# Hybrid decoder step on one core: keys and attention queries transposed two heads at a time instead of from doubled copies

## The chip, the core and the metric

The kernel runs on 1 core of one Trainium2 chip. The time is device microseconds (us) of one execution of the whole program. Five engines work side by side and wait for one another only through semaphores: TensorE (PE, with its weight loads shown apart as PEld), VectorE (DVE), ScalarE (ACT), GpSimd (POOL) and SyncE (SP, which here only issues DMAs). Each runs its own instructions strictly in the order in which they stand.

## The reference

One decoder layer for a prompt of 2048 tokens and 8 decode sequences of 8 tokens. What matters here is the attention of the prompt: 8 query heads and 4 key/value heads of 64 dimensions, so two query heads share a key head.

```python
def sparse_attend(q, kg, vg, valid):
    qg = q.reshape(B, T, N_KV_HEADS, N_HEADS // N_KV_HEADS, HEAD_DIM)
    s = jnp.einsum('btgrd,btkgd->btgrk', qg, kg, ...) * HEAD_DIM ** -0.5
    s = jnp.where(valid[:, :, None, None, :], s, -jnp.inf)
    p = jax.nn.softmax(s, axis=-1).astype(vg.dtype)
    o = jnp.einsum('btgrk,btkgd->btgrd', p, vg)
...
    score = indexer_scores(qib, wb, ki)          # 8 indexer heads, one shared key
    idx, valid = select_keys(score, posb, k_top) # 256 best causal keys of each query
    return sparse_attend(qb, take(k, idx), take(v, idx), valid)
```

The kernel computes the attention densely over all causal keys and adds a mask that leaves the selected ones. Around it stand the input projection, a gated position mixing, the output projection and a last gated projection.

## The kernel before

The program has three stages. **Stage A** (`phase_a`, 0 to about 1026 us) projects the 17 blocks of 128 tokens, scores and selects keys (the indexer) and, at its end, multiplies the gated mixing by one half of the output weights (`gm_product`, lines 585 to 589, 34 products). **Stage B** (`phase_b`, about 1026 to 1516 us) is the attention of the prompt; the decode sequences' attention is mixed in between as filler. **Stage C** (`phase_c`, to the end) is the output projection and the gated one behind it.

All products are in float32r with the operands split in a high part and a low part (`split`, lines 124 to 127: ACT copies the high part out of PSUM, DVE subtracts it to get the low part). For the scores the split is laid over the partitions: a head has 64 dimensions, TensorE has 128 rows. `Kst` holds for each key head the high part of the transposed keys in partitions 0 to 63 and the low part in 64 to 127. A transposed query head stands in both halves, so one matmul multiplies it with the high and the low part of the keys together: `b_qh` is the high part of the query doubled, `b_ql` its low part doubled (lines 1117 and 1118).

To have every head doubled, the kernel before transposes inputs that are doubled already. `load_q` (line 1009) reads the 128x512 queries of a block twice into `b_qr`, in pieces of 64 numbers, so that each head's 64 columns stand there twice; `prep_q` (line 1043) then makes 8 transposes of 128x128 into two PSUM banks and splits each bank. `twice` (line 1027) lets ACT copy a block of keys doubled into `b_kd`; `prep_kv` (line 1031) makes 4 transposes into one bank, ACT copies the bank to `Kst`, DVE replaces the lower half by the difference; POOL splits the values into `Vst`. Key and value blocks are loaded two ahead (pool `b_raw` with two buffers).

`prep_early` prepares the queries of block 0 and all 16 key blocks while the last products of stage A run on PE. In stage B a block i of queries is worked in four steps g = 0 to 3, one per key head, each with two heads: `scores` (matmuls into the pool `b_s` of two banks, then DVE adds the mask and takes the running extreme, ACT exponentiates) and, one step later, `values` (transposes of the probabilities into the pool `b_tp` of four banks, a split by ACT and DVE into `b_pt`, then the product with `Vst`). The queries of the next block are prepared at the end of step g = 2, in banks of the same pool `b_tp`, and the load of the block after it is issued right there. Between the stages A and B stands a conditional block (`fallback`, line 915) that every engine has to pass.

The order on each engine is set by a scheduler when the program is built: it plays the program with its own estimate of durations and puts down what is ready. The code above gives it dependencies and priorities; on the chip each engine keeps to that order.

## Time and profile before

| | |
|---|---|
| runs | 1872.78, 1873.06, 1878.46 us; median 1873.06 us |
| profiled execution | 1874.53 us, of it 1872.7 us span from the first to the last instruction |
| mean granted TensorE clock | 0.991 of 2.4 GHz |
| busy, share of the span | PE 97%, PEld 85%, DVE 66%, ACT 54%, POOL 32% |
| DMA | 261.54 MB in all |
| stage B, 1050 to 1520 us | PE 459.80, DVE 411.86, ACT 373.44, POOL 153.29 of 470 us |

A share is an average over stages that differ: DVE is 66% busy over the span, and 88% in stage B. A matmul's listed duration is longer than the step from one to the next, since they are pipelined; what a matmul costs PE is read from the start of the next one. An engine's idle time is put down to the event that ended it.

### The profile page before, as it was taken

The page shows a single profiled execution, that of the slowest core. Times are in us where ns is not written, and L with a number is a line of the kernel's source. Part 1 is how long each engine was busy: PE and PEld are TensorE (multiplying, and loading weights), DVE is VectorE, ACT ScalarE, POOL GpSimd, SP SyncE. Part 2 cuts the span into 40 slices and gives each one's busy share as a digit, 9 for nine tenths or more (in the row PEclk, how much of TensorE's full clock was granted, in tenths as well). Part 3 has the DMA queues.
Part 4 walks back from the last instruction along what each step waited for, and adds up shares of the span by engine and source line. Part 5 has one row for each costly group of instructions (what it writes and reads, how often), then busy time and mean ns, then how long its engine had stood idle before and what let it go on. Part 6 is the DMA issues. An engine that isn't in the chain of part 4 may idle for free. (4 is left out here: it accounts for less than half of the span.)

```text
span 1872.7 us, 33926 instructions
## 1 busy us (share of the span) xinstructions
PE 1821.9 (97%) x11974; PEld 1599.1 (85%) x11974; DVE 1243.2 (66%) x3638; ACT 1019.7 (54%) x1912; POOL 608.2 (32%) x967
## 2 busy tenths in 40 slices
PE   7998999999999999999999899999999999999998
PEld 6997978999999999998988777788778878888887
DVE  4588753568788638768754788899979974233321
ACT  3234434446656636677665888688867753122121
POOL 4566362433013325004403642522234113222221
PEclk9998999999999999999999899999999999999999
DMA  8854665645445564454455551522133063223211
GB/s 241 283 182 145 212 204 188 212 126 157 127 154 167 201 185 144 142 169 154 151 195 169 144 138 49 157 63 72 54 87 116 12 226 109 75 96 107 93 37 46
DMA packets 243807, 261.54 MB, mean 140 GB/s; under 512 B 83177, under 2 KB 209841, under 8 KB 243249
## 3 DMA queue, kind: packets, MB, share of 16 engines
q1 hardware_dynamic: 147200, 144.10, 24.8%
q10 hardware_dynamic: 90544, 96.35, 15.8%
q0 software_dynamic: 5888, 18.88, 3.5%
q8 instruction: 95, 1.56, 0.3%
q14 instruction: 80, 0.65, 0.1%
HBM read 171.90 MB, written 87.37 MB: 138 GB/s over the span
## 5 line engine op out<-in xcount | busy, mean ns | idle before, releaser
L323 PE MATMUL z<-whi,hhi 128*128 128x256 f32 (+1 forms) x1792 | 463.4, 292 | 7.6 <-ACT qn L397 2.6
L324 PE MATMUL z<-wlo,hhi 128*128 128x256 f32 (+1 forms) x1792 | 454.4, 287 | 1.3 <-DVE wlo L293 1.3
L323 PEld LDWEIGHTS z<-whi,hhi 128*128 128x128 f32 x1792 | 342.1, 191 | 17.2 <-ACT qn L397 3.6
L324 PEld LDWEIGHTS z<-wlo,hhi 128*128 128x128 f32 x1792 | 342.4, 191 | 6.5 <-DVE wlo L293 1.5
L326 PE MATMUL z<-whi,hlo 128*128 128x256 f32 (+1 forms) x1792 | 262.1, 285 | 0.0
L326 PEld LDWEIGHTS z<-whi,hlo 128*128 128x128 f32 x1792 | 237.9, 189 | 2.2
L706 DVE SCALAR_TENSOR_TENSOR big<-dots,sgn,big 128x1024 f32<-128x1024 f32 (+7 forms) x176 | 179.0, 1017 | 48.2 <-ACT dots L704 43.1
L127 DVE TENSOR_TENSOR b_pt<-b_tp,b_pt 128x512 fp32r<-128x512 f32 (+1 forms) x288 | 183.3, 655 | 12.8 <-ACT b_pt L126 11.7
L1169 PE MATMUL b_o<-b_pt,Vst 128*128 128x512 f32 x544 | 184.0, 421 | 1.3 <-DVE b_pt L127 1.3
L704 ACT ACTIVATE dots<-dots 128x1024 f32<-128x1024 f32 (+7 forms) x176 | 139.7, 800 | 82.3 <-PE dots L702 78.5
L126 ACT ACTIVATE b_pt<-b_tp 128x512 fp32r<-128x512 f32 (+1 forms) x288 | 156.5, 579 | 43.2 <-PE b_tp L1152 39.3
L1152 PE MATMUL b_tp<-mats,b_sm 128*128 128x128 f32 x1088 | 170.8, 275 | 1.6 <-ACT b_sm L1126 0.7
L843 ACT ACTIVATE bfw<-big,tk 128x384 bf16<-128x384 f32 (+14 forms) x105 | 136.5, 1300 | 60.3 <-DVE tk L863 34.9
L1126 ACT ACTIVATE b_sm<-b_sm,b_st 128x128 f32<-128x128 f32 (+15 forms) x128 | 154.9, 1211 | 24.3 <-DVE b_st L1119 23.6
L1152 PEld LDWEIGHTS b_tp<-mats,b_sm 128*128 128x128 f32 x1088 | 132.3, 141 | 31.0 <-ACT b_sm L1126 3.3
L1117 PE MATMUL b_s<-Kst,b_qh 128*128 128x512 f32 (+3 forms) x320 | 138.3, 435 | 5.1 <-DVE b_st L1119 4.3
L1119 DVE CUSTOM_DVE_ANT_0 b_sm<-b_s,b_mask,b_st 128x512 f32<-128x512 f32 (+3 forms) x192 | 123.8, 645 | 18.4 <-PE b_s L1118 13.9
L701 PE MATMUL dots<-ki_stack,qih 128*128 128x512 f32 (+3 forms) x304 | 113.1, 373 | 3.4 <-DVE big L706 1.8
L1118 PE MATMUL b_s<-Kst,b_ql 128*128 128x512 f32 (+3 forms) x320 | 116.4, 368 | 0.0
L702 PE MATMUL dots<-ki_stack,qil 128*128 128x512 f32 (+3 forms) x304 | 109.4, 369 | 0.0
L1169 PEld LDWEIGHTS b_o<-b_pt,Vst 128*128 128x128 f32 x544 | 91.0, 190 | 20.9 <-DVE b_pt L127 5.5
L1484 PE MATMUL c_mm<-c_h_w_ple_gate,c_mh 128*128 128x512 f32 x272 | 108.8, 400 | 0.0
(349 smaller groups left out, 3742.7 us busy)
## 6 DMA issues: line engine op xcount, KB each, us to landing
whi<-s_wh ACTq DMA_DIRECT2D x52, 512.0 KB
wlo<-s_wl ACTq DMA_DIRECT2D x52, 512.0 KB
raw<-w_in SPq DMA_DIRECT2D x112, 128.0 KB
s_wh<-whi ACTq DMA_DIRECT2D x13, 1024.0 KB
s_wl<-wlo ACTq DMA_DIRECT2D x13, 1024.0 KB
s_r<-hlo SPq DMA_DIRECT2D x32, 256.0 KB
b_qr<-s_q SPq DMA_DIRECT2D x32, 256.0 KB
c_r<-s_r SPq DMA_DIRECT2D x16, 512.0 KB
```

Source lines behind the costliest of these rows:

```text
L126: nc.scalar.activation(hi, src, AF.Copy)
L127: nc.vector.tensor_tensor(lo, src, hi.bitcast(F32), OP.subtract)
L323: nc.tensor.matmul(z, lhsT=hh[:, k], rhs=wh[:, k, :n], start=(k == 0), stop=False)
L324: nc.tensor.matmul(z, lhsT=hh[:, k], rhs=wl[:, k, :n], start=False, stop=False)
L326: nc.tensor.matmul(z, lhsT=hl[:, k], rhs=wh[:, k, :n], start=False, stop=(k == 7))
L704: nc.scalar.activation(r, r, AF.Relu)
L706: nc.vector.scalar_tensor_tensor(a, r, self.sgn[:, b, h:h + 1], a, op0=OP.mult, op1=OP.add)
L843: nc.scalar.activation(junk, acc[:P], AF.Sign, bias=cur[:, 0:1], accum_out=cur[:, 1:2])
L1117: nc.tensor.matmul(ps, lhsT=qh[:, h], rhs=rhs, start=True, stop=False)
L1126: nc.scalar.activation(part, part, AF.Exp, bias=stt[:, h, c:c + 1], scale=-1.0, accum_out=stt[:, h, 4 + e:5 + e])
L1152: nc.tensor.transpose(ps[:, k, r], sm2[r][:, (k0 + k) * 128:(k0 + k) * 128 + 128], ident)
L1169: nc.tensor.matmul(o.rearrange("p a b -> p (a b)"), lhsT=Vst[:, kb, g].rearrange("p a d -> p (a d)"), rhs=pt[:, k].rearrange("p a b -> p ( ...
```

## The change

Heads are no longer doubled ahead of the transposes. A transpose of 128 columns takes two heads at once: the first comes out in partitions 0 to 63, the second in 64 to 127. The doubling is done behind it, by copies that cross the halves:

- Queries (`prep_q`, new function `heads`): one load of 128x512 in whole rows, 4 transposes into one bank. For each of the two heads of a pair (e = 0, 1) ACT copies 64x512 to the head's own half of `b_qh`, DVE subtracts to the own half of `b_ql`, ACT copies the same source to the other half of `b_qh`, and the other half of `b_ql` is made by DVE out of the bank for blocks 0 to 4, and by POOL as a copy in SBUF for blocks 5 to 15. That is 4 ACT instructions of 64x512 for 2 of 128x512, and 4 or 2 DVE instructions of 64x512 for 2 of 128x512, and 0 or 2 on POOL.
- Keys (`prep_kv`): 2 transposes of the loaded keys, no doubled copy. For an even key head the high part stays in the upper half, for an odd one in the lower; ACT copies 64x256 and DVE subtracts 64x256, each twice per block.
- Key and value blocks are loaded four ahead (pool `b_raw` with four buffers).
- The queries of the next block are prepared at the end of step g = 0 instead of g = 2, and with them the load of the block after it is issued two steps earlier.
- The indexer's heads are transposed doubled, as before.

```diff
--- before.py
+++ after.py
@@ -44,6 +44,8 @@
 KIN = 4
 LAG_SM = 4
 LEAD = 2
+QR = 1
+AHEAD = 4
 SPS = 0
 SY = 8
 X_POOL = 0
@@ -673,6 +675,20 @@
             n = min(512, W - c)
             self.nc.gpsimd.tensor_scalar(acc[:P, c:c + n], self.iota[:P, :n], float(c), -UNIT, op0=OP.add, op1=OP.mult)
 
+    def heads(self, pool, names, ps, bufs, direct):
+        nc = self.nc
+        qh, ql = (pool.tile([128, 2, 4, 128], F32R, name=n, bufs=bufs) for n in names)
+        own = [slice(0, 64), slice(64, 128)]
+        for e in range(2):
+            nc.scalar.activation(qh[own[e], e], ps[own[e]], AF.Copy)
+            nc.vector.tensor_tensor(ql[own[e], e], ps[own[e]], qh[own[e], e].bitcast(F32), OP.subtract)
+            nc.scalar.activation(qh[own[1 - e], e], ps[own[e]], AF.Copy)
+            if direct:
+                nc.vector.tensor_tensor(ql[own[1 - e], e], ps[own[e]], qh[own[e], e].bitcast(F32), OP.subtract)
+            else:
+                nc.gpsimd.tensor_scalar(ql[own[1 - e], e], ql[own[e], e].bitcast(F32), 1.0, 1.0, op0=OP.mult, op1=OP.mult)
+        return qh, ql
+
     def idx(self, b):
         nc, wk, wk2 = self.nc, self.wk, self.wk2
         W = 128 * (b + 1)
@@ -988,7 +1004,7 @@
         qp = pool("b_q", 2)
         tiny = pool("b_tiny", 3)
         er = ExitStack()
-        raw = er.enter_context(tc.tile_pool(name="b_raw", bufs=2, reuse_waits="tile", side="right"))
+        raw = er.enter_context(tc.tile_pool(name="b_raw", bufs=AHEAD, reuse_waits="tile", side="right"))
         Kst = self.Kst = [kv.tile([128, 4, 512], F32R, name=f"Kst{c}") for c in range(4)]
         Vst = self.Vst = kv.tile([128, NB, 4, 2, 64], F32R, name="Vst")
         cm = kv.tile([128, 256], BF, name="cm")
@@ -1007,10 +1023,9 @@
             kvs[i] = (k, v)
 
         def load_q(i):
-            q = io.tile([128, 8, 2, 64], F32, name="b_qr", bufs=1)
+            q = io.tile([128, 4, 128], F32, name="b_qr", bufs=QR)
             ga = io.tile([128, 512], F32, name="b_ga")
-            for a in range(2):
-                nc.sync.dma_start(q[:, :, a], self.s_q[i].rearrange("t (h d) -> t h d", h=8))
+            nc.sync.dma_start(q, self.s_q[i].rearrange("t (h d) -> t h d", h=4))
             nc.sync.dma_start(ga, self.s_ga[i])
             qs[i] = (q, ga)
 
@@ -1022,39 +1037,32 @@
             else:
                 self.ms[i] = cm[:, 256 - W:]
 
-        kds = {}
-
-        def twice(i):
-            kds[i] = raw.tile([128, 4, 2, 64], F32, name="b_kd")
-            nc.scalar.copy(kds[i], kvs[i][0].rearrange("p (h d) -> p h d", h=4)[:, :, None, :].to_broadcast([128, 4, 2, 64]))
-
         def prep_kv(i, psum):
-            k, v = kds.pop(i), kvs.pop(i)[1]
+            k, v = kvs.pop(i)
             ps = psum()
-            for g in range(4):
-                nc.tensor.transpose(ps[:, g], k[:, g].rearrange("p a d -> p (a d)"), ident)
-            ks = Kst[i // 4][:, :, (i % 4) * 128:(i % 4) * 128 + 128]
-            nc.scalar.activation(ks, ps, AF.Copy)
-            V.tensor_tensor(ks[64:128], ps[64:128], ks[64:128].bitcast(F32), OP.subtract)
+            for j in range(2):
+                nc.tensor.transpose(ps[:, j], k[:, j * 128:j * 128 + 128], ident)
+            ks = Kst[i // 4].rearrange("p (j e) n -> p j e n", e=2)[:, :, :, (i % 4) * 128:(i % 4) * 128 + 128]
+            own = [slice(0, 64), slice(64, 128)]
+            for e in range(2):
+                nc.scalar.activation(ks[own[e], :, e], ps[own[e], 0:2], AF.Copy)
+                V.tensor_tensor(ks[own[1 - e], :, e], ps[own[e], 0:2], ks[own[e], :, e].bitcast(F32), OP.subtract)
             vv = v.rearrange("p (g d) -> p g d", g=4)
             nc.gpsimd.tensor_scalar(Vst[:, i, :, 0], vv, 1.0, 1.0, op0=OP.mult, op1=OP.mult)
             nc.gpsimd.tensor_tensor(Vst[:, i, :, 1], vv, Vst[:, i, :, 0].bitcast(F32), OP.subtract)
 
         def prep_q(i, psum):
             q, ga = qs.pop(i)
-            qh = qp.tile([128, 8, 128], F32R, name="b_qh")
-            ql = qp.tile([128, 8, 128], F32R, name="b_ql")
-            for j in range(2):
-                ps = psum()
-                for h in range(4):
-                    nc.tensor.transpose(ps[:, h], q[:, j * 4 + h].rearrange("p a d -> p (a d)"), ident)
-                self.split(qh[:, j * 4:j * 4 + 4], ql[:, j * 4:j * 4 + 4], ps)
+            ps = psum()
+            for j in range(4):
+                nc.tensor.transpose(ps[:, j], q[:, j], ident)
+            qh, ql = self.heads(qp, ("b_qh", "b_ql"), ps, 2, i < 5)
             stt = tiny.tile([128, 8, 6], F32, name="b_st")
             self.prs[i] = (qh, ql, ga, stt)
 
         self.load_q, self.load_mask, self.prep_q = load_q, load_mask, prep_q
-        load_kv(0)
-        load_kv(1)
+        for i in range(AHEAD):
+            load_kv(i)
         load_q(ORDER[0])
         for b in ORDER[:2]:
             if b < 2:
@@ -1062,14 +1070,11 @@
         yield
         prep_q(ORDER[0], psum)
         load_q(ORDER[1])
-        twice(0)
         yield
         for i in range(NB):
-            if i + 1 < NB:
-                twice(i + 1)
             prep_kv(i, psum)
-            if i + 2 < NB:
-                load_kv(i + 2)
+            if i + AHEAD < NB:
+                load_kv(i + AHEAD)
             yield
         er.close()
 
@@ -1110,12 +1115,12 @@
                         sm = both[:, r, :W]
                     out.append(sm)
 
-                    def chunk(c, h=h, sm=sm):
+                    def chunk(c, h=h, sm=sm, r=r):
                         c0, cn = c * 512, min(512, W - c * 512)
                         ps = sp.tile([128, 512], F32, name="b_s")[:, :cn]
                         rhs = Kst[c][:, g, :cn]
-                        nc.tensor.matmul(ps, lhsT=qh[:, h], rhs=rhs, start=True, stop=False)
-                        nc.tensor.matmul(ps, lhsT=ql[:, h], rhs=rhs, start=False, stop=True)
+                        nc.tensor.matmul(ps, lhsT=qh[:, r, g], rhs=rhs, start=True, stop=False)
+                        nc.tensor.matmul(ps, lhsT=ql[:, r, g], rhs=rhs, start=False, stop=True)
                         V.tensor_tensor_reduce(out=sm[:, c0:c0 + cn], in0=ps, in1=m[:, c0:c0 + cn], scale=1.0,
                                                scalar=3.0e38 if c == 0 else stt[:, h, c - 1:c], op0=OP.add, op1=OP.min,
                                                accum_out=stt[:, h, c:c + 1])
@@ -1239,7 +1244,7 @@
                         while fill_n >= 1:
                             fill_n -= 1
                             next(fill, None)
-                if si < len(steps) and g == 2 and at + 1 < NB:
+                if si < len(steps) and g == 0 and at + 1 < NB:
                     self.prep_q(ORDER[at + 1], psum)
                     if at + 2 < NB:
                         self.load_q(ORDER[at + 2])
```

In the built program 96 transposes less stand on PE: 32 of keys and 64 of queries. In these rows of the orders an x and a number count equal instructions in a row, and the brackets name the engines or DMA queues waited for.

PE, in the last products of stage A (`z`), where two key blocks are transposed between two products; before:

```order
L589 MATMUL z<-whi,hhi 128x512 x4
L1035 MATMUL dots<-mats,b_kd 128x128 [waits DVE_49,Activation_49]
L1035 MATMUL dots<-mats,b_kd 128x128 x3
L1035 MATMUL dots<-mats,b_kd 128x128 [waits DVE_49,Activation_49]
L1035 MATMUL dots<-mats,b_kd 128x128 x3
L585 MATMUL z<-whi,hhi 128x512 [waits Activation_49]
```

and now:

```order
L591 MATMUL z<-whi,hhi 128x512 x4
L1044 MATMUL dots<-mats,b_kr 128x128 [waits DMAHW7_49,DVE_49,PE_49]
L1044 MATMUL dots<-mats,b_kr 128x128
L1044 MATMUL dots<-mats,b_kr 128x128 [waits DMAHW0_49,DVE_49,PE_49]
L1044 MATMUL dots<-mats,b_kr 128x128
L587 MATMUL z<-whi,hhi 128x512 [waits Activation_49]
```

Four transposes of the doubled copy `b_kd` for each block have become two of the loaded keys `b_kr`, and PE waits for the load itself (a DMA queue) where it waited for ACT's copy.

PE, at the start of stage B, where the queries of block 2 are prepared (`b_s`: scores, `b_tp`: transposes, `b_o`: products with the values); before, 35 rows behind those of block 1:

```order
L1282 MATMUL b_tp<-mats,s_pg 128x64 [waits DMAHW7_49]
L1282 MATMUL b_tp<-mats,s_pg 128x64
L1050 MATMUL b_tp<-mats,b_qr 128x128 [waits DMAHW0_49,DMAHW1_49,DVE_49,PE_49]
L1050 MATMUL b_tp<-mats,b_qr 128x128 x3
L1152 MATMUL b_tp<-mats,b_sm 128x128 [waits Activation_49]
```

and now, from the last scores of block 0 to both preparations:

```order
L1122 MATMUL b_s<-Kst_12929,b_qh 128x128 [waits DVE_49]
L1123 MATMUL b_s<-Kst_12929,b_ql 128x128
L1058 MATMUL b_tp<-mats,b_qr 128x128 [waits DVE_49,PE_49]
L1058 MATMUL b_tp<-mats,b_qr 128x128 x3
L1157 MATMUL b_tp<-mats,b_sm 128x128 [waits DVE_49,PE_49]
L1157 MATMUL b_tp<-mats,b_sm 128x128 [waits Activation_49] x5
L1174 MATMUL b_o<-b_pt,Vst 128x512 [waits DVE_49,Pool_49]
L1157 MATMUL b_tp<-mats,b_sm 128x128 [waits PE_49]
L1157 MATMUL b_tp<-mats,b_sm 128x128
L1174 MATMUL b_o<-b_pt,Vst 128x512 [waits DVE_49]
L1058 MATMUL b_tp<-mats,b_qr 128x128 [waits DMAHW4_49,PE_49]
L1058 MATMUL b_tp<-mats,b_qr 128x128 x3
```

The queries of block 2, which are loaded into the same buffer as those of block 1, are now transposed six rows behind those of block 1.

ACT, in block 9 of stage B, where the queries of block 10 are split; before:

```order
L1320 ACTIVATE s_kT<-b_tp 128x256 [waits PE_49]
L126 ACTIVATE b_qh<-b_tp 128x512 [waits PE_49]
L1126 ACTIVATE b_sm,b_st<-b_sm,b_st 128x1280 [waits DVE_49]
L126 ACTIVATE b_qh<-b_tp 128x512 [waits PE_49]
L1185 ACTIVATE b_x<-b_o 128x256 [waits PE_49]
L126 ACTIVATE b_pt<-b_tp 128x2x256 [waits PE_49,Activation_49] x2
```

and now:

```order
L128 ACTIVATE b_pt<-b_tp 128x256 [waits DVE_49,PE_49]
L683 ACTIVATE b_qh<-b_tp 64x512 [waits PE_49]
L685 ACTIVATE b_qh<-b_tp 64x512 [waits DVE_49]
L1190 ACTIVATE b_x<-b_o 128x256 [waits PE_49]
L683 ACTIVATE b_qh<-b_tp 64x512
L1131 ACTIVATE b_sm,b_st<-b_sm,b_st 128x1280 [waits DVE_49]
L1201 ACTIVATE b_mix<-b_o 128x256 [waits DVE_49,PE_49,Pool_49]
L685 ACTIVATE b_qh<-b_tp 64x512 [waits DVE_49]
L128 ACTIVATE b_pt<-b_tp 128x2x256 [waits PE_49,Activation_49] x2
```

Two copies that waited for PE alone have become four, and two of them wait for DVE.

## Rows read from the trace of the kernel before

**Rows 1.** The page: the span, PE's busy time, and the granted clock in 40 equal slices of the span (9 is 90% or more).

```profile
span 1872.7 us, 33926 instructions
...
PE 1821.9 (97%) x11974; PEld 1599.1 (85%) x11974; DVE 1243.2 (66%) x3638; ACT 1019.7 (54%) x1912; POOL 608.2 (32%) x967
...
PEclk9998999999999999999999899999999999999999
```

**Rows 2.** The view by stretches of the span: the stretch and its length, busy us (and instructions) of PE, PEld, DVE, ACT and POOL, granted clock, share of the DMA engines, GB/s.

```profile
965.00:990.00 25.00, 25.00 (x126) 20.96 (x125) 15.42 (x66) 16.94 (x27) 0.00 (x0) 1.00 0.54 174
...
1050.00:1520.00 470.00, 459.80 (x3072) 365.53 (x3072) 411.86 (x1106) 373.44 (x750) 153.29 (x251) 1.00 0.31 87
1520.00:1872.70 352.70, 345.91 (x1627) 284.41 (x1625) 123.05 (x140) 82.90 (x134) 84.73 (x63) 1.00 0.29 98
```

**Rows 3.** The timeline of PE at the 8 transposes of block 0's queries in stage A: start, us from the start of the first to the end of the last, line, operation, count.

```profile
959.21 1.07 PE L589 MATMUL z<-whi,hhi 128*128 128x512 f32 x4
960.12 1.03 PE L1050 MATMUL dots<-mats,b_qr 128*128 128x128 f32 x8
960.91 0.48 PE L585 MATMUL z<-whi,hhi 128*128 128x512 f32 x1
```

**Rows 4.** The timeline of PE from the last product of stage A into stage B; in brackets the idle time ahead of an instruction and what ended it.

```profile
1025.27 0.39 PE L586 MATMUL z<-wlo,hhi 128*128 128x512 f32 x1
...
1033.15 0.48 PE L1117 MATMUL b_s<-Kst,b_qh 128*128 128x128 f32 x1 [2.43 <-DVE b_st L1119]
...
1035.20 1.11 PE L1152 MATMUL b_tp<-mats,b_sm 128*128 128x128 f32 x4 [0.31 <-DVE Kst L1038]
1036.11 1.91 PE L1050 MATMUL b_tp<-mats,b_qr 128*128 128x128 f32 x8
1037.68 0.78 PE L1169 MATMUL b_o<-b_pt,Vst 128*128 128x512 f32 x1
...
1045.65 1.09 PE L1050 MATMUL b_tp<-mats,b_qr 128*128 128x128 f32 x4 [1.84 <-DMA b_qr<-s_q]
```

**Rows 5.** The timeline of DVE there: the first instruction behind the conditional block, and the last key block's difference.

```profile
1032.65 0.17 DVE L1199 RECIPROCAL b_st<-b_st 128x2 f32<-128x2 f32 x1 [3.11 <-DVEq L917]
...
1034.45 0.69 DVE L1038 TENSOR_TENSOR Kst<-dots,Kst 64x512 fp32r<-64x512 f32 x1
```

**Rows 6.** The chain of waits that ended last, three of its pieces: start, us, what the chain was in.

```profile
1038.67 6.84 DMA b_qr<-s_q
...
1078.82 0.44 PE b_tp L1050 x4
...
1097.62 0.44 PE b_tp L1050 x4
```

**Rows 7.** The view by stretches again, in steps of 4 us around the change of stages (columns as in Rows 2).

```profile
1028.00:1032.00 4.00, 2.20 (x16) 1.70 (x15) 1.48 (x9) 3.97 (x12) 0.00 (x0) 0.97 0.27 63
1032.00:1036.00 4.00, 2.17 (x8) 1.80 (x9) 2.78 (x13) 2.07 (x10) 2.76 (x4) 0.50 0.41 84
1036.00:1040.00 4.00, 3.95 (x22) 3.46 (x20) 3.02 (x8) 3.00 (x9) 3.09 (x4) 0.68 0.73 228
...
1044.00:1048.00 4.00, 2.35 (x11) 2.38 (x12) 2.55 (x11) 1.40 (x5) 1.77 (x3) 0.68 0.52 156
1048.00:1052.00 4.00, 4.00 (x28) 3.75 (x27) 3.36 (x13) 4.00 (x14) 2.31 (x6) 0.90 0.28 63
1052.00:1056.00 4.00, 4.00 (x31) 3.75 (x30) 4.00 (x16) 4.00 (x14) 2.61 (x4) 1.00 0.79 214
```

**Rows 8.** The views by tile: the instructions that write or read one tile, with the shortest, median and longest duration in ns, first and last start, and shapes.

```profile
L126 ACT ACTIVATE b_qh<-b_tp x30: 577/597/753, 1037.2 to 1450.8; 128x512 fp32r<-128x512 f32 x30
L127 DVE TENSOR_TENSOR b_ql<-b_tp,b_qh x30: 666/685/693, 1037.8 to 1452.7; 128x512 fp32r<-128x512 f32 x30
...
L1029 ACT COPY b_kd<-b_kr x16: 606/620/630, 954.5 to 1027.7; 128x512 f32<-128x512 f32 x16
...
L1038 DVE TENSOR_TENSOR Kst<-dots,Kst x16: 686/694/695, 993.5 to 1034.5; 64x512 fp32r<-64x512 f32 x16
...
L1185 ACT ACTIVATE b_x<-b_o x64: 359/383/477, 1038.6 to 1515.5; 128x256 f32<-128x256 f32 x64
...
L1040 POOL TENSOR_SCALAR Vst<-b_vr x16: 403/404/406, 992.3 to 1019.5; 128x256 fp32r<-128x256 f32 x16
```

**Rows 9.** The timeline of ACT and DVE at the split of block 3's queries, two banks.

```profile
1061.88 1.23 ACT L126 ACTIVATE b_qh<-b_tp 128x512 fp32r<-128x512 f32 x2
...
1062.66 1.29 DVE L127 TENSOR_TENSOR b_ql<-b_tp,b_qh 128x512 fp32r<-128x512 f32 x2 [0.61 <-ACT b_qh L126]
```

**Rows 10.** The view by stretches in steps of 20 us, three early and three late ones of stage B (columns as in Rows 2).

```profile
1050.00:1070.00 20.00, 19.23 (x121) 14.52 (x121) 15.85 (x47) 18.05 (x56) 12.41 (x25) 1.00 0.58 155
1070.00:1090.00 20.00, 19.66 (x141) 15.80 (x139) 16.68 (x49) 18.37 (x52) 11.48 (x22) 1.00 0.50 136
1090.00:1110.00 20.00, 19.84 (x138) 15.80 (x137) 17.57 (x56) 17.49 (x45) 8.68 (x16) 1.00 0.44 123
...
1410.00:1430.00 20.00, 19.61 (x114) 15.52 (x113) 19.14 (x51) 14.76 (x24) 14.94 (x12) 1.00 0.62 195
1430.00:1450.00 20.00, 19.95 (x123) 16.70 (x122) 19.38 (x49) 16.25 (x26) 3.37 (x8) 1.00 0.16 54
...
1470.00:1490.00 20.00, 20.00 (x120) 16.48 (x119) 19.29 (x49) 15.79 (x25) 1.72 (x4) 1.00 0.09 27
```

## The prediction, made before the changed kernel ran

> **What bounds the kernel now.** I read the page first. PE is busy 1821.9 of 1872.7 us, and its clock was granted in full but for two slices [rows 1]. An average hides stages, so I went on to the stretches. At the end of stage A, where the key blocks are prepared, PE is busy 25.00 of 25 us; in stage B 459.80 of 470 beside DVE with 411.86 and ACT with 373.44; in stage C 345.91 of 352.70 [rows 2]. So an instruction less on PE is worth its step wherever PE doesn't wait, and stage B has two engines that stand close behind it. PE waits in one place: in the 10 us behind stage A's last product [rows 4]. DVE is held there for 3.11 us by the conditional block [rows 5], PE waits 2.43 for DVE and later 1.84 for the queries of block 2, whose load was under way for 6.84 us [rows 4, 6]. The clock there is 0.50, then 0.68, and full again from 1052 on [rows 7].
>
> **Stage A.** A transpose of 128 columns at full clock takes 0.79 us / 8 = 0.099 us (960.12 to 960.91) [rows 3]. The change saves 4 transposes of block 0's queries and 32 of keys. Those of key blocks 12 to 15 stand behind the last product, where PE waits for DVE anyway; blocks 0 to 11 and the queries make 24 + 4 = 28 x 0.099 = 2.8 us. Will the cheaper order on the other engines take it back? ACT loses the doubled copy (0.62) and the full copy (about 0.60) per block and gets two of 64x256. DVE loses one of 64x512 (0.69) and gets two of 64x256. The rows say that halving the partitions saves nothing (64x512 takes 694 ns where 128x512 takes 685) and that 256 columns take 383 on ACT [rows 8]. For DVE's 256 columns I estimate 694 x 383/597 = 0.45. So ACT goes from 1.22 to 0.77 us per block, DVE from 0.69 to 0.89. DVE is busy 15.42 of 25 us there [rows 2]; the 0.2 has room. PE also waits for the load itself now, which is four blocks ahead. **Term: -2.8.** Bounds: -3.6 if the other 8 count too; 0 if the last products end at the pace of DVE, which the 25.00 speaks against.
>
> **The change of stages.** PE's first products of stage B wait for DVE, which waits for the conditional block; transposes less ahead of that shorten nothing. Behind it the 8 transposes of block 1's queries take 1.57 us (1036.11 to 1037.68) at a low clock [rows 4]; 4 would take 0.8, a gain of 0.8. Against it: block 2's queries are now transposed six rows behind block 1's, out of the same buffer, so the load starts when block 1's transposes end and PE wants it some 2.5 us later (three groups of transposes and two products by the steps of rows 4). The load was under way for 6.84 us [rows 6]; it moves half the bytes now, so from 3.4 to 6.84. PE would wait 0.9 to 4.3 there, in place of the 1.84 of before, that is -0.9 to +2.5. In a sentence apart: the Trainium skill (DMA: Bandwidth & Descriptors, Specifications) wants at least 512 B in a transfer for the full rate, and the load before moves pieces of 256 B where the new one moves whole rows of 2 KB; by that the load would be at the short end or below. The row gives only the 6.84 of the short pieces. With the 0.8: **term 0**, bounds -3.5 (the wait goes, and with it the low clock around it) to +3 (PE waits longest, and the clock stays low longer).
>
> **Queries of blocks 1 to 4.** In stage B four transposes take 0.44 us [rows 6], 0.11 each. 16 less: -1.8. For it ACT gets four instructions of 64x512 for two of 128x512, and by rows 8 each costs the same 0.60: +1.2 per block, +4.8 in all. DVE gets four for two, +1.4 per block, +5.5 in all. ACT has no room there: 4.00 of 4 us in 1048 to 1056 [rows 7], then 18.05, 18.37, 17.49 of 20 [rows 10]. PE keeps 19.23 to 19.84 of 20 beside it. Both can't be passed on in full, since they overlap; taken is a little over half of ACT's cost against PE's saving: 2.8 - 1.8 = **+1.0**, bounds -1.8 (all hidden) to +5.5 - 1.8 = +3.7, and +5.5 if the saving is lost too.
>
> **Queries of blocks 5 to 15.** 44 transposes less: -4.8. ACT's +1.2 per block has room (14.76 to 16.25 of 20 [rows 10]). DVE's count stays at two, of 64x512 (0.69) instead of 128x512 (0.685) [rows 8]: no change. But DVE is at 19.14 to 19.38 of 20 [rows 10], the second bound there. POOL gets two copies of 64x512 per block; 128x256 takes it 404 ns [rows 8], so 0.4 to 0.8 each, where it has 5 to 18 idle us in 20 [rows 10]. Their result is needed by the scores of the next block, three steps later now that the work stands at g = 0; a block takes some 470/16 = 29 us. If that cover were gone, the price is the chain: 4 x 0.60 + 2 x 0.69 + 0.8 = 4.6 us per block. SP issues one load of queries for two; the next one still waits for PE's transposes, and behind it in SP's queue stand only a mask and a gate block for a later step, a block ahead of use. The loads of key blocks that are moved four ahead are 2 of 128x256 each in stage A, on a DMA share of 0.54 [rows 2]: nothing. **Term: -4.4**, bounds -4.8 to +1 (DVE sets the pace at the end of the stage).
>
> **Sum.** -2.8 + 0 + 1.0 - 4.4 = -6.2. The profiled execution took 1874.53 (1872.7 span and 1.8 around it): 1868.3. The median of the runs is 1.5 lower at 1873.06, so the forecast is 1866.9, 0.33% faster. 0.3%, which is about what a measurement of this kernel can tell from no change, is 5.6 us: faster means below 1867.4, slower above 1878.7. The forecast lies at that edge.
>
> **Rivals.**
>
> A: **the saving is absorbed** by ACT early and DVE late. For it: DVE at 19.3 of 20 [rows 10], and probabilities and queries go through the same two engines. Against it: PE is at 19.6 to 20.00 of 20 in the same stretches, so it isn't waiting now. The time: the late term halves to -2.2 and blocks 1 to 4 cost +2.6: -2.8 + 2.6 - 2.2 = -2.4, 1870.7.
>
> B: **slower, by one bank's chain.** Before, two banks were split side by side: ACT and DVE were done 2.07 us from the start (1061.88 to 1063.95) [rows 9]. Now one bank is read by ACT, DVE, ACT for each half of the partitions, and ACT stands in wait for DVE; queued behind it on ACT are the copies of the probabilities (`b_pt`) that PE wants next. The bank is held 4 x 0.60 + 2 x 0.69 = 3.8 us from block 5 on, 5.2 for blocks 1 to 4, if all go in turn. It is one of the four banks of `b_tp` through which the probabilities pass. If PE loses the 1.3 us of one DVE subtraction and one copy per block, 15 x 1.3 = 19.5 against 9.4 saved on PE (2.8, 1.8 and 4.8): +10, 1883. It ends even at 9.4/15 = 0.63 us per block, and is slower by over 0.3% from 15.0/15 = 1.0 on. Against it: two banks were taken before, one now, so three are left for the probabilities, and the second half's ACT copy stands free of DVE's wait in the new order. The Trainium skill (PSUM — Partial Sum Buffer, "PSUM bank collisions raise a hardware error") forbids two engines the same bank and quadrant of 32 partitions at once, reads included; the order's waits on DVE agree, and by the same section the halves of 64 don't bar each other, by which the chain would be nearer 2.6 to 3.8 us. No row here shows two engines in one bank.
>
> C: **the change of stages gains more.** Half the bytes in longer pieces land in time: the wait of 1.84 goes, and the low clock around it (0.68 in 1044 to 1048 and 0.90 in the next [rows 7]), (1 - 0.68) x 4 + 0.1 x 4 = 1.7 us: -3.5 more, 1863.4. Against it: the load is wanted sooner after its issue.
>
> D: **PE waits for block 2's queries** at the low clock, near the long end: 4.3 in place of 1.84, less the 0.8, and another 4 us at 0.68 (1.3): +3.0 over the forecast, 1869.9. For it: six rows lie between the two preparations; the landing is the only row that there is.
>
> **How the numbers follow.** Forecast 0.44, held between 1862.5 and 1871 (0.27 of it below 1867.4), C 0.20, A 0.18, D 0.08, B 0.10. Faster by over 0.3%: 0.27 + 0.20 = 0.47; within 0.3%: 0.17 + 0.18 + 0.08 = 0.43; slower: B, 0.10. The range reaches from C with blocks 1 to 4 at -1.8 and blocks 5 to 15 at -4.8 (1863.4 - 2.8 - 0.4, so 1860) to A with +3.7 and +1 for them (1870.7 + 1.1 + 3.2 = 1875.0); B is left out.
>
> **What would show it.** In the timeline of PE four transposes with one step of 0.44 for block i; a total of 96 matmuls less and PE busy about 9 us less. In stage A the last product ends near 1022.5 in place of 1025.7: right if so, DVE's pace if not. If block 2's transposes are preceded by an idle time put down to a DMA of over 2 us, D; with none, C. If PE in 1050 to 1110 is busy less than 19 of 20 with the idle time put down to ACT or DVE (`b_pt`), A; if such waits stand beside every preparation through 1490, B. The forecast is wrong if DVE sits at 20 of 20 at the end of stage B and PE waits for `b_sm`, or if the second half of `b_ql` by POOL is what PE's scores wait for.

## The result and the profile after

The changed kernel takes 1886.58 us (median of 5 runs, 1885.94 to 1887.22) where the kernel before took 1872.94 beside it (5 runs): a ratio of 1.0063, with an interval from 1.0052 to 1.0074. It is slower by some 12 us, where 1866.9 was forecast; the forecast and its range both missed.

The page of the profiled execution, span, busy times and granted clock in 40 slices, answers to [rows 1]:

```profile
span 1885.5 us, 33801 instructions
...
PE 1826.6 (97%) x11878; PEld 1592.3 (84%) x11878; DVE 1255.9 (67%) x3664; ACT 1034.5 (55%) x1944; POOL 625.5 (33%) x989
...
PEclk8999999999999999999998899999999999999999
```

PE has its 96 matmuls less (11974 to 11878), and is busy 4.7 us longer. To see where, the span is cut at three events that both kernels have: the first product of `gm_product`, the end of its last one, and the end of the last product of stage B. The view by stretches, columns as in [rows 2]; before:

```profile
913.84:1025.66 111.82, 111.82 (x551) 92.47 (x550) 63.44 (x200) 71.63 (x115) 26.86 (x48) 1.00 0.53 174
1025.66:1516.80 491.14, 475.24 (x3164) 379.12 (x3163) 427.07 (x1171) 390.77 (x801) 163.95 (x269) 0.99 0.31 88
1516.80:1872.67 355.87, 348.33 (x1638) 286.22 (x1636) 124.76 (x142) 83.88 (x136) 85.99 (x65) 1.00 0.30 100
```

and the changed kernel:

```profile
914.26:1023.15 108.89, 108.89 (x521) 88.92 (x519) 65.51 (x212) 67.15 (x115) 26.09 (x48) 1.00 0.53 173
1023.15:1526.28 503.13, 479.52 (x3097) 372.57 (x3097) 435.66 (x1184) 409.17 (x834) 178.64 (x291) 0.98 0.26 79
1526.28:1885.45 359.17, 349.67 (x1639) 287.39 (x1636) 124.73 (x142) 83.91 (x136) 86.27 (x65) 0.99 0.29 99
```

Ahead of them 0.42 us more, then 111.82 to 108.89 (-2.93), 491.14 to 503.13 (+11.99), 355.87 to 359.17 (+3.30): the sum is the 12.8 us of the spans. I call the three stretches **products**, **attention** and **end**. In the attention PE has 67 recorded matmuls less and is idle for 23.6 us in place of 15.9. How well one profile measures a stretch: two kernels below with the same instructions up to the end of the attention (the changed one and `c_order`) differ there by 1.65 us; the start of the products lies anywhere from 911.5 to 916.6 in the kernels below, which are all alike up to near there. So a stretch tells more than the span, and 2 us of attention tell nothing.

At the change of stages, PE's timeline, answering to [rows 4], and below it two pieces of the chain:

```profile
1022.76 0.39 PE L588 MATMUL z<-wlo,hhi 128*128 128x512 f32 x1
...
1031.71 0.47 PE L1122 MATMUL b_s<-Kst,b_qh 128*128 128x128 f32 x1 [2.49 <-DVE b_st L1124]
...
1033.34 1.09 PE L1058 MATMUL b_tp<-mats,b_qr 128*128 128x128 f32 x4 [0.51 <-DVE Kst L1049]
...
1040.21 1.09 PE L1058 MATMUL b_tp<-mats,b_qr 128*128 128x128 f32 x4 [2.34 <-DMA b_qr<-s_q]
```

```profile
1034.64 5.44 DMA b_qr<-s_q
1040.21 1.10 PE b_tp L1058 x4
```

The queries of block 2 are loaded in 5.44 us where it was 6.84 [rows 6], but wanted earlier: PE waits 2.34 in place of 1.84. The clock, by the view by stretches, stays at 0.50, the lower of its two levels, for 16 us (and is 0.93 and 0.60 in the next two slices). The kernel before had one such slice of 4 us, and was back at 1.00 from 1040 to 1044, a slice that [rows 7] leaves out:

```profile
1028.00:1032.00 4.00, 1.51 (x8) 1.32 (x7) 1.20 (x8) 2.21 (x10) 1.01 (x3) 0.50 0.16 40
1032.00:1036.00 4.00, 3.21 (x14) 2.50 (x13) 3.01 (x11) 3.49 (x13) 3.08 (x4) 0.50 0.69 179
1036.00:1040.00 4.00, 1.62 (x4) 0.96 (x4) 3.37 (x8) 2.48 (x6) 3.54 (x7) 0.50 0.89 302
1040.00:1044.00 4.00, 3.77 (x15) 3.07 (x15) 2.08 (x6) 2.60 (x7) 0.90 (x3) 0.50 0.44 139
```

The prices of the copies, from the views by tile, answer to [rows 8]:

```profile
L683 ACT ACTIVATE b_qh<-b_tp x30: 583/592/613, 1034.5 to 1440.2; 64x512 fp32r<-64x512 f32 x30
L684 DVE TENSOR_TENSOR b_ql<-b_tp,b_qh x30: 673/689/695, 1035.1 to 1440.9; 64x512 fp32r<-64x512 f32 x30
L685 ACT ACTIVATE b_qh<-b_tp x30: 589/593/599, 1036.2 to 1442.7; 64x512 fp32r<-64x512 f32 x30
...
L689 POOL TENSOR_SCALAR b_ql<-b_ql x22: 612/616/621, 1094.6 to 1442.1; 64x512 fp32r<-64x512 f32 x22
```

So each instruction costs what the prediction took (0.60, 0.69, 0.4 to 0.8). What it did not see is what they do to PE. One row of the page's groups shows a part of it, PE's first matmul of the scores; behind the bar its busy time, mean ns and the idle time ahead of it. Before:

```profile
L1117 PE MATMUL b_s<-Kst,b_qh 128*128 128x512 f32 (+3 forms) x320 | 138.3, 435 | 5.1 <-DVE b_st L1119 4.3
```

and after:

```profile
L1122 PE MATMUL b_s<-Kst,b_qh 128*128 128x512 f32 (+3 forms) x320 | 140.3, 440 | 8.5 <-DVE b_st L1124 7.7
```

The scores wait for DVE to read the last ones out of their two banks, 7.7 us in place of 4.3. The views by stretches that answer to [rows 10] have PE below what it was, early in stage B (19.23 and 19.66 there) and less so late in it (19.95 and 20.00 there), beside a DVE that is nearly as busy late:

```profile
1050.00:1070.00 20.00, 18.23 (x111) 13.15 (x109) 16.87 (x53) 19.00 (x58) 12.82 (x25) 0.97 0.37 114
1070.00:1090.00 20.00, 18.84 (x112) 13.92 (x112) 17.27 (x48) 17.84 (x48) 9.43 (x18) 1.00 0.34 112
...
1430.00:1450.00 20.00, 19.50 (x118) 15.94 (x117) 19.14 (x47) 17.79 (x29) 13.36 (x14) 1.00 0.45 135
1470.00:1490.00 20.00, 19.60 (x116) 15.95 (x115) 18.68 (x47) 16.20 (x26) 2.34 (x6) 1.00 0.00 0
```

These slices stand at the same times, but the changed kernel is up to some 12 us behind there. To compare the same work, the attention is cut at two more events, the first scores of block 2 and the first scores of block 10; before:

```profile
1025.66:1050.42 24.76, 18.28 (x107) 15.73 (x106) 17.23 (x67) 18.73 (x56) 12.34 (x22) 0.79 0.51 134
1050.42:1245.82 195.40, 191.42 (x1338) 151.62 (x1336) 167.67 (x483) 163.48 (x381) 83.07 (x142) 1.00 0.40 111
1245.82:1516.80 270.98, 265.54 (x1725) 211.77 (x1724) 242.18 (x623) 208.56 (x366) 68.54 (x106) 1.00 0.23 67
```

and the changed kernel:

```profile
1023.15:1052.44 29.29, 19.42 (x88) 15.03 (x88) 20.85 (x73) 20.68 (x59) 12.00 (x21) 0.65 0.38 112
1052.44:1256.08 203.64, 195.48 (x1312) 148.79 (x1312) 172.46 (x491) 174.46 (x402) 91.29 (x155) 1.00 0.31 94
1256.08:1526.28 270.20, 264.62 (x1701) 208.75 (x1700) 242.35 (x622) 214.03 (x375) 75.35 (x117) 1.00 0.20 64
```

I call the three pieces the **change** of stages, the **middle** and the **late** part. They are 4.5 and 8.2 us longer and 0.8 shorter: all of the loss falls ahead of block 10's first scores. (The middle of `c_order`, with the same instructions, takes 206.1, 2.5 more; so much lies between two executions.)

### The profile page after: what moved, and what is told of

Read it like the earlier page. It is cut to its first block, busy times and chain, and to the rows that moved or that the text cites. A ratio compares the mean times of both kernels' runs of the same rounds, so it can differ in the third digit from the quotient of the medians.

```text
span 1885.5 us, 33801 instructions
## 1 busy us (share of the span) xinstructions
PE 1826.6 (97%) x11878; PEld 1592.3 (84%) x11878; DVE 1255.9 (67%) x3664; ACT 1034.5 (55%) x1944; POOL 625.5 (33%) x989
## 5 line engine op out<-in xcount | busy, mean ns | idle before, releaser
L1489 PE MATMUL c_mm<-c_h_w_ple_gate,c_mh 128*128 128x512 f32 x272 | 108.7, 400 | 0.0
```

Source lines behind the costliest of these rows:

```text
L1489: nc.tensor.matmul(z, lhsT=hi[:, k], rhs=wts[k][0][:, ns], start=(k == 0), stop=False)
```

## The experiments

Four theories of the 12 us in the attention: the **bank** (rival B: the one bank of the queries is held too long), the **work** (ACT's two instructions more per block, DVE's two more in blocks 1 to 4), the **place** (g = 0, with the wait for block 2's queries), and that the saving **can't be cashed** since DVE and ACT set the pace. The last two runs decide the last one. All ratios are to the kernel before.

| kernel | ratio | interval | products | attention | end |
|---|---|---|---|---|---|
| before | 1 | | 111.8 | 491.1 | 355.9 |
| changed | 1.0063 | 1.0052 to 1.0074 | 108.9 | 503.1 | 359.2 |
| k_only | 0.9996 | 0.9984 to 1.0008 | 109.3 | 490.9 | 357.0 |
| q_only | 1.0075 | 1.0052 to 1.0099 | 112.9 | 502.3 | 356.8 |
| b_early | 1.0002 | 0.9993 to 1.0012 | 111.8 | 490.1 | 355.9 |
| q_late | 1.0072 | 1.0047 to 1.0096 | 108.9 | 503.8 | 357.6 |
| qr2 | 1.0053 | 1.0036 to 1.0069 | 108.8 | 498.5 | 359.3 |
| sbuf_act | 1.0057 | 1.0039 to 1.0076 | 109.3 | 501.2 | 355.8 |
| act_sbuf | 1.0041 | 1.0027 to 1.0056 | 108.7 | 500.8 | 355.8 |
| no_direct | 1.0059 | 1.0040 to 1.0079 | 108.8 | 504.8 | 357.5 |
| act2 | 1.0018 | 1.0008 to 1.0028 | 108.9 | 495.9 | 360.2 |
| pool4 | 1.0028 | 1.0016 to 1.0041 | 108.7 | 498.9 | 360.3 |
| pool4_qr2 | 1.0016 | 1.0002 to 1.0030 | 109.4 | 498.0 | 358.9 |
| act2_qr2 | 1.0038 | 1.0025 to 1.0050 | 111.1 | 497.4 | 357.4 |
| mix_qr2 | 1.0020 | 1.0011 to 1.0030 | 108.9 | 495.2 | 355.8 |
| act_more | 1.0033 | 1.0022 to 1.0043 | 112.1 | 493.8 | 359.3 |
| c_order | 1.0052 | 1.0035 to 1.0070 | 109.2 | 504.8 | 355.5 |
| k_early | 1.0008 | 0.9999 to 1.0018 | 109.3 | 492.2 | 358.9 |
| k_half | 0.9964 | 0.9954 to 0.9974 | 108.9 | 484.1 | 355.8 |
| b_half | 0.9979 | 0.9970 to 0.9989 | 111.4 | 487.1 | 357.4 |

**One part alone.** `k_only` has the hunk of `prep_kv` and the loads four ahead, with `load_q`, `prep_q` and g == 2 as before; `q_only` has the hunks of `load_q`, `heads`, `prep_q` and g == 0, with `twice` and `prep_kv` as before.

> The part on the keys alone (two transposes per key block, copies across the halves, loads four ahead); the queries are doubled, prepared at g = 2 and split in two banks as before. Four stretches of the span are compared: stage A to its last product (1025.66 before, 1023.15 in the changed kernel), from there to the first scores of block 2 (24.8 before, 29.3 changed), from there to the last product of stage B (466.1 and 473.6), and from there to the end (356.1 and 359.4). If the loss lies in the queries alone, as each of the theories on bank, work and place has it: stage A -2.5, the two next stretches as before, some 1870.4. If the keys' part disturbs the change of stages too, the second stretch stays above 26.

> The part on the queries alone (one load, four transposes, copies across the halves, prepared at g = 0); the keys are doubled by ACT as before. If the loss lies in the queries: stage A -0.4, second stretch 28 to 30, third 473 to 475, in all 1883 to 1889. If it comes from keys and queries together, nearer to 1876.

The loss is all in the queries: 490.9 against 502.3. The keys' part takes 2.5 us off the products and nothing else; in the whole time that is not told from no change.

**The place.** One line each way, in the changed kernel (`q_late`, shown) and in the one before (`b_early`, the other way round):

```diff
-                if si < len(steps) and g == 0 and at + 1 < NB:
+                if si < len(steps) and g == 2 and at + 1 < NB:
```

> The changed kernel with the queries prepared at the end of g = 2, as before the change. Theory of the place: the second stretch falls to 25 to 26, since block 2's load is wanted later, and the third by 1 to 3. Theories of bank and work: the third stretch stays within 2 us of 473.6, or grows, since POOL's copies have one step less to be done in.

> The kernel before with only the place changed: its doubled queries are prepared at the end of g = 0 (8 transposes, two banks, splits of 128x512). Theory of the place: the second stretch grows from 24.8 to 28 to 30 with a wait for the load of block 2, and the third by 2 to 7. Theories of bank and work: the second grows by the wait for the load at most, and the third stays within 1.5 us of 466.1.

503.8 with the place undone and 490.1 with the place alone: the move as such costs nothing that can be measured. The wait for block 2's queries may cost something. `qr2` takes it away:

```diff
-QR = 1
+QR = 2
```

> The changed kernel with two buffers for the loaded queries (b_qr), so that the load of block 2 need not wait for the transposes of block 1. The wait of 2.34 us for that load goes. If it was on the path: the second stretch falls from 29.3 to 26 to 27. If DVE or ACT are late there anyway: by less than 1, and another wait stands in its place.

The attention falls by 4.6, of it 3.1 in the change of stages (29.3 to 26.2); the time falls too, but its interval overlaps that of the changed kernel. Two pairs below differ in this buffer alone, and with it the attention is 1.0 shorter (`pool4_qr2` against `pool4`) and 1.5 longer (`act2_qr2` against `act2`). So a gain from the second buffer is not shown.

**The bank.** `sbuf_act` makes both other halves from SBUF, so that the bank is read by two instructions of ACT and two of DVE alone:

```diff
-            nc.scalar.activation(qh[own[1 - e], e], ps[own[e]], AF.Copy)
+            nc.scalar.activation(qh[own[1 - e], e], qh[own[e], e].bitcast(F32), AF.Copy)
...
-                nc.vector.tensor_tensor(ql[own[1 - e], e], ps[own[e]], qh[own[e], e].bitcast(F32), OP.subtract)
+                nc.vector.tensor_scalar(ql[own[1 - e], e], ql[own[e], e].bitcast(F32), 1.0, 1.0, op0=OP.mult, op1=OP.mult)
```

> The changed kernel, but the other half is made from the own half in SBUF and not from the bank: ACT copies b_qh, DVE (blocks 0 to 4) or POOL copies b_ql. As many instructions of the same sizes on each engine; the bank is free after two instructions of ACT and two of DVE in place of four and two or four. Theory of the bank (one of the four banks of b_tp is held for 8.4 us per block on average, and the transposes of the probabilities wait for it): the third stretch falls by 4 to 7 us. Theory of the work (ACT's two instructions more per block, DVE's two more in blocks 1 to 4, have no room): it stays within 1.5 us of 473.6. Theory of the place (g = 0 in place of g = 2): it stays as well.

From the first transpose of a block's queries to the end of the bank's last reader, read off the timelines of PE, ACT and DVE, it was some 8.4 us on average over 15 blocks in the changed kernel, and is 5.8 here; the attention falls by 1.9, about what two executions differ by, and none of it in the middle (205.95, where the changed kernel takes 203.64). The theory of the bank falls as the main cause. `act_sbuf` has the first of these two replacements alone:

> The changed kernel, but ACT's second copy of b_qh reads the own half in SBUF and not the bank; all else as changed (four copies of ACT, DVE's second subtraction out of the bank in blocks 0 to 4). The copy then no longer waits for DVE's subtraction, and holds nothing back on ACT. Measured from the last product of stage A to the last one of stage B: 491.1 before, 503.1 changed, 495.9 without ACT's second copies, 493.8 with two such copies added to the kernel before. If the wait for DVE in ACT's queue is what the second copies cost: 494 to 498. If the copies' time is: 501 to 504.

500.8: that ACT waits for DVE between its copies is not the main cost either.

**The work.** `act2` moves ACT's second copy to POOL, `no_direct` DVE's second subtraction of blocks 0 to 4 (`i < 5` becomes `False`), `pool4` both. The line of `act2`:

```diff
-            nc.scalar.activation(qh[own[1 - e], e], ps[own[e]], AF.Copy)
+            nc.gpsimd.tensor_scalar(qh[own[1 - e], e], qh[own[e], e].bitcast(F32), 1.0, 1.0, op0=OP.mult, op1=OP.mult)
```

> The changed kernel with only ACT's second copy taken away: POOL copies b_qh to the other half in SBUF, b_ql is made as in the changed kernel (by DVE from the bank in blocks 0 to 4, by POOL behind). Stretch from the last product of stage A to the first scores of block 10, 232.9 changed, 226.6 with all four copies on POOL. If ACT's two instructions are the cost: 226 to 228. If DVE's two more in blocks 1 to 4 are: 231 to 233.

> The changed kernel with DVE's second subtraction taken away in blocks 0 to 4: POOL copies b_ql there too; ACT's four copies stay. Same stretch. If DVE's two more are the cost (8 x 0.69 = 5.5 us): 227 to 229. If ACT's are: 231 to 233.

> The changed kernel, but both other halves are copied from the own halves in SBUF by POOL, for all blocks: per block 2 instructions of ACT and 2 of DVE (as many as before the change) and 4 of POOL of 0.62 us. Theories of the bank and of the work: both causes are gone, the third stretch falls from 473.6 to 462 to 466, unless POOL's copies come late for the scores of the next block. The theory of the place: the second stretch stays at 29, the third too.

ACT's second copies are the one edit that tells: 503.1 to 495.9, and a ratio of 1.0018 whose interval lies apart from that of the changed kernel. DVE's subtractions tell nothing (504.8). `pool4`, which takes both away, comes to 470.1 behind the first scores of block 2, where 462 to 466 was expected: a part of the loss lies elsewhere.

The pieces of the attention say where. In the middle, eight kernels in which ACT makes the second copies (the changed one, `c_order`, `q_only`, `q_late`, `qr2`, `sbuf_act`, `act_sbuf`, `no_direct`) take 202.7 to 207.1 us, and five in which POOL makes them there (`act2`, `act2_qr2`, `pool4`, `pool4_qr2`, `mix_qr2`) 196.2 to 197.6. Late, it is 269.7 to 271.7 against 271.5 to 272.5. The middle and the late part of `act2`:

```profile
1049.75:1245.99 196.24, 190.75 (x1301) 147.20 (x1300) 169.42 (x485) 163.07 (x379) 99.25 (x167) 1.00 0.32 98
1245.99:1517.65 271.66, 265.90 (x1704) 209.48 (x1703) 242.42 (x623) 208.36 (x366) 81.62 (x127) 1.00 0.21 63
```

So with ACT's second copies the middle, where ACT was busy 84% before the change, is some 7 us longer than with POOL's; late, where it was busy 77%, they are no dearer than POOL's.

`act_more` adds two such instructions of ACT to the kernel before:

```diff
+            for n in range(2):
+                spare = tiny.tile([128, 4, 128], F32, name="b_spare", bufs=1)
+                nc.scalar.activation(spare[64 * n:64 * n + 64], qh[64 * n:64 * n + 64, 0:4].bitcast(F32), AF.Copy)
```

> The kernel before, with two more ACT copies of 64x512 per block from b_qh into a tile that nobody reads: the two instructions of ACT that the change adds, and nothing else of it (8 transposes, two banks, g = 2). Measured from the last product of stage A to the first scores of block 10, where the changed kernel takes 232.9 against 220.2 us, and behind it to the last product of stage B (270.2 against 271.0). Theory of the work: ACT's idle time in the first of them stays about 38 us, so the ten blocks prepared in it add most of 10 x 1.2 = 12 us: 228 to 232. Rival, the order of the waits (ACT stands in wait for DVE between its copies and holds back what is queued behind): these copies wait for nothing, so 220 to 223.

Its attention, whole and in the three pieces:

```profile
1024.39:1518.22 493.83, 480.81 (x3165) 376.55 (x3163) 427.02 (x1170) 406.88 (x831) 164.13 (x269) 1.00 0.31 88
...
1024.39:1046.33 21.94, 16.01 (x104) 13.24 (x101) 15.47 (x64) 18.68 (x55) 12.03 (x21) 0.92 0.59 151
1046.33:1246.05 199.72, 196.69 (x1335) 150.91 (x1334) 168.04 (x484) 173.10 (x399) 83.20 (x141) 1.00 0.40 109
1246.05:1518.22 272.17, 268.11 (x1733) 212.40 (x1732) 243.52 (x624) 215.10 (x380) 68.90 (x107) 1.00 0.23 67
```

ACT is busy 406.88 us, 16 more than before and 2 less than in the changed kernel, and the stretch is 2.7 us longer, not 12. So ACT's work by itself is no full account. To the first scores of block 10 it takes 221.7, which the expectation gives to the order of the waits. But 2.7 is not the price of the two copies: the change of stages came out 2.8 shorter, at a clock of 0.92 where it was 0.79, and the two parts behind it 5.5 longer (471.9 in place of 466.4). The other three kernels with doubled queries and all transposes (`k_only`, `b_early`, `k_early`) take 467.2 to 469.2 there. So the two copies cost some 3 to 5.5 us there, and in the changed kernel some 6: the eight kernels named above take 472.3 to 477.2 behind the change of stages, the five 467.9 to 470.1. That the same work costs less in the kernel before is not shown. (By time `act_more` loses 6; 3.5 of it lie in the end, of which below.)

**Together.** `pool4_qr2` and `act2_qr2` join the second buffer to these; `mix_qr2` lets ACT and DVE make the other halves in blocks 0 to 2, and POOL behind:

> All four copies to the other halves on POOL, and two buffers for the loaded queries. If the 6 us by which the first of the two alone is still above 220.2 are the wait for block 2's queries and the low clock behind it: 221 to 224. If they are POOL's copies that come late: 226 as without the second buffer. In all 1873 to 1876 if the former.

> Two of the edits that gained, together: POOL makes the second copies of b_qh, and b_qr has two buffers. The stretch from the last product of stage A to the last of stage B: if the two gains (7.2 and 4.6 us) are apart from each other, 491 to 493, as before the change, and with stage A's 2.9 in all 1870 to 1873 if stage C is 356. If POOL is late at the start of stage B, where it issues the decode sequences' indirect loads, 495 to 497.

> The copies by place: ACT and DVE make the other halves in blocks 0 to 2 (where POOL is busy with the indirect loads of the decode sequences, and PE waited 1.66 us for its copy), POOL makes both in blocks 3 to 15; two buffers for b_qr. If POOL's lateness at the start and ACT's load behind it are what is left: 488 to 492 for the same stretch, in all 1868 to 1872. If the four transposes less can't be cashed in stage B at all, because DVE and ACT set its pace: 491 or more.

The gains don't add up: 498.0, 497.4, 495.2. In `pool4_qr2` PE now waits for POOL at the start of block 1, as its timeline shows, with POOL in the indirect loads of the decode sequences until 1038.5:

```profile
1043.91 0.80 PE L1119 MATMUL b_s<-Kst,b_qh 128*128 128x256 f32 x2 [1.66 <-POOL b_qh L685]
```

`mix_qr2` avoids that and has the shortest attention of those with four transposes and all of the copies; it stays 4 us above the kernel before. By time, `act2`, `pool4_qr2` and `mix_qr2` are not told apart. `k_early` (the keys' part and g == 0 with doubled queries) was to be the best of all:

> The keys' part of the change alone, and the doubled queries prepared at the end of g = 0. Stage A's products with their transposes take 109 us in place of 111.8 (as with the keys' part alone), the stretch behind them 490 to 491 (as with either edit alone): in all 1869 to 1871, faster than both. If the two edits collide at the change of stages: 1873 to 1876.

It is the same as the kernel before, within its interval: no version here that computes everything beats that one.

**The end of the program.** The profile of the changed kernel has this on ACT, and PE behind it:

```profile
1540.99 1.06 ACT L1440 ACTIVATE c_h_w_ple_gate<-c_raw 128x1024 fp32r<-128x1024 f32 x1 [4.84 <-DMA c_raw<-w_ple_gate]
1541.95 1.07 ACT L128 ACTIVATE c_oh<-c_tp 128x512 fp32r<-128x512 f32 x2
```

```profile
1542.58 0.72 PE L1489 MATMUL c_mm<-c_h_w_out,c_oh 128*128 128x512 f32 x1 [2.41 <-ACT c_oh L128]
```

In the kernel before the copies `c_oh` stand ahead of that weight block. No line of stage C is changed; the scheduler, whose own clock for stage B had moved, put them in the other order. `c_order` binds it, with the two instructions kept by name:

```diff
+            tc.add_manual_dep(acts['w_ple_gate', 3].ins, ohs[blocks[3]].ins.name, mybir.DependencyInfo(mybir.DependencyClass.NoSync, mybir.DependencyReason.DATA), reason='order')
```

> The changed kernel with one order added in stage C: ACT makes the high part of the fourth block of gate weights behind the copies c_oh of the third and fourth block of mixings, as in the kernel before, and not ahead of them. If that swap of places cost the 3.3 us in the last stretch (ACT stood 4.84 us in wait for a load of weights, and PE 2.41 us for ACT): the last stretch falls from 359.4 to some 356, all else stays, 1883.3. If the stretch is longer for another reason, no change.

```profile
1529.61:1885.15 355.54, 348.13 (x1638) 286.26 (x1636) 123.55 (x142) 83.77 (x136) 83.94 (x65) 0.99 0.29 100
```

The end is back at 355.5, and PE's wait of 2.41 us for `c_oh` is 0.7; so that order is the 3.3 us of this profile, as far as one pair of profiles can say. In time the gain of `c_order` is within the intervals. The table shows ends of 358.9 to 360.3 in six more kernels. Of these `qr2` has the same order; in the traces of the other five, `act_more` among them, the copies `c_oh` stand ahead of the weight block as in the kernel before. So a long end has other causes too, and no run here tells which.

**The saving alone.** `k_half` is `k_only`, `b_half` is `b_early`, with half of the queries' transposes left out:

```diff
-                for h in range(4):
+                for h in range(2):
...
-                self.split(qh[:, j * 4:j * 4 + 4], ql[:, j * 4:j * 4 + 4], ps)
+                pair = lambda t: t.rearrange("p (a b) n -> p a b n", a=2)
+                self.split(pair(qh[:, j * 4:j * 4 + 4]), pair(ql[:, j * 4:j * 4 + 4]), ps[:, None, 0:2].to_broadcast([128, 2, 2, 128]))
```

> The keys' part alone, with doubled queries at g = 2, and half of the queries' transposes left out: per bank the third and fourth transpose are not made, and the splits by ACT and DVE (128x512 as before) read the first two heads' columns twice, so that half of the query heads are wrong. PE does 64 transposes less, as in the changed kernel, and no other engine does anything more. From the last product of stage A to the last of stage B: 490.9 with all transposes. If PE sets the pace of stage B, as the prediction has it: 60 x 0.11 = 6.6 less, 484 to 485, in all some 1867. If DVE and ACT set it and the saving can't be cashed: 489 to 491.

> The same on the kernel before with its queries prepared at g = 0: half of the queries' transposes left out, the splits read the first two heads' columns twice, half of the query heads are wrong. 490.1 with all transposes. PE sets the pace: 483 to 484. DVE and ACT do: 488 to 490.

`k_half` in the attention, by stretches:

```profile
1023.11:1507.23 484.12, 470.84 (x3097) 369.87 (x3097) 425.71 (x1176) 389.23 (x804) 164.01 (x269) 0.99 0.31 89
```

`k_half` takes 6.8 us less than `k_only`, and `b_half` 2.9 less than `b_early`, for 6.6 us of transposes. Behind the change of stages the two agree better: 467.2 to 461.9 and 469.2 to 463.1, that is 5.3 and 6.2 less for 13 blocks x 0.44 = 5.7; in the change itself `b_half` happens to be 3.2 longer. PE sets the pace of stage B, and the saving is real. With it and the keys' part the kernel takes 1864.85 us, close to what was forecast. What the change puts in the place of the four transposes turns 484.1 into 503.1: 22.2 to 29.3 in the change of stages, 193.3 to 203.6 in the middle, 268.6 to 270.2 late. The middle and the late part of `k_half`:

```profile
1045.34:1238.60 193.26, 190.42 (x1314) 148.33 (x1313) 167.43 (x488) 163.86 (x384) 83.99 (x143) 1.00 0.40 113
1238.60:1507.23 268.63, 264.43 (x1701) 209.09 (x1700) 241.61 (x622) 207.27 (x365) 68.04 (x106) 1.00 0.23 68
```

## Why the prediction was wrong

- **Stage A, -2.8: right.** The products take 2.93 less, and 2.5 less with the keys' part alone; the last one ends at 1023.15 where 1022.5 was said.
- **What bounds the kernel: right.** Both runs on the saving alone have it in the time: a ratio of 0.9964 and 0.9979. The rival A, that DVE and ACT absorb what PE saves, falls as a rule for the stage. Its sign for the early blocks, PE under 19 of 20 us, did come (18.23 and 18.84); late PE is idle for 5.6 us, where it was 5.4.
- **The change of stages, 0 within -3.5 and +3: the size was off.** The wait for block 2's queries came as in rival D, 2.34 us with a landing of 5.44, in the middle of the bounds given, and the clock stayed low longer. Without the wait the attention is 4.6 us shorter in one profile, and the time says -1.9 with overlapping intervals; in the other two pairs it is 1.0 shorter and 1.5 longer. So the wait's price lies somewhere from 0 to 4.6, and the piece as a whole is 4.5 us longer than before.
- **The step that failed is the price of the copies in the queries' two terms**: "a little over half of ACT's cost against PE's saving", +1.0 for blocks 1 to 4, and "ACT's +1.2 per block has room" for blocks 5 to 15, -4.4. The saving under these terms was right (6.6). The price of the copies was taken as 3.2 (2.8 and 0.4); what stands in the transposes' place, with the wait above, cost 503.1 - 484.1 = 19.0 us, of it 7.1 in the change of stages, 10.4 in the middle and 1.6 late. So "has room" held in the late part and failed ahead of block 10. The 14.76 to 16.25 of 20 that it rests on are slices from 1410 on; in block 6 of the kernel before, ACT is busy 19.19 of 20:

```profile
1130.00:1150.00 20.00, 20.00 (x125) 16.79 (x123) 18.21 (x53) 19.19 (x45) 5.81 (x12) 1.00 0.26 69
```

- **Rival B had that price** (1.3 per block, 19.5 in all, 1883 us) **by luck.** Holding the bank 2.6 us less per block gave back 1.9, no more than two executions differ by, and the loss does not stand beside every preparation through 1490, as B has it: only 1.6 of the 19.0 is late.
- **What is shown of the cause**: ACT's second copies (7.2 us of attention, 8 by the ratios) are the largest part that one edit takes away, and thirteen kernels agree that they cost some 7 us more than POOL's in the middle, and no more late.
- **What stays open**: 11 us between `mix_qr2` and `k_half`, of it 3.8 in the change of stages, 4.3 in the middle and 2.9 late. They differ in splits of 64 partitions in place of 128, in POOL's four copies per block, in one bank in place of two, in the load, in the place, and in the order that the scheduler makes of all this; no run here tells these apart. Nor is it shown by which wait ACT's copies reach PE: in the middle of the changed kernel the waits of one line of PE for one line of another engine add up to 1.2 us at most.
- **The end, +3.3, was not in the prediction**: by `c_order` it is an order in stage C that the scheduler changed, but five kernels have as long an end without that order.

## What to carry to other kernels

Before a cheaper form is built, run the saving alone, with nothing in its place: it gives the ceiling (here 7 to 8 us with the keys' part), and the distance to it is the price of what was put there. Judge an engine's room where the new work will stand, and not from other slices of the same stage: ACT's second copies were no dearer than POOL's where ACT had been busy 77%, and some 7 us dearer where it had been busy 84%. Work that PE saves at 0.1 us apiece was bought there with instructions of 0.6 us on engines that PE waits for. Where a scheduler makes the order, cut the time into stages at fixed events: an edit in one stage can reorder another, and here the last stretch, which no edit but `c_order` touches, took from 355.5 to 360.3 us.

## What the runs showed of the hardware

- An instruction over 64 partitions cost what one over 128 costs: 592 ns for ACT's 64x512 against 597 [rows 8], 689 for DVE's against 685.
- Half the bytes in rows of 2 KB landed in 5.44 us where the doubled load in pieces of 256 B took 6.84. That is one load each, beside other traffic, and no run changes the size of the pieces alone. The 3.4 of the prediction, by the halved bytes, was far off. The Trainium skill (DMA: Bandwidth & Descriptors, Specifications) asks for transfers of at least 512 B for the full rate; by that it would have been at the short end, and the measurement decides that here it was not.
- The granted clock was 0.50 for 16 us at the change of stages where PE was busy 1.51 to 3.77 of every 4 us, against one slice of 4 us at 0.50 in the kernel before. Over the whole change of stages it was 0.65 against 0.79, and 0.92 in `act_more`.
